# A hybrid DeltaNet and gMLP step: where the scan scales its operands, how its triangular inverse is joined, and how the modulation sums are laid on the array

## The chip, the cores and the metric

The kernel runs on one core of one Trainium2 chip. The metric is the device time of one execution in microseconds (us); less is better. The engines are named as the profile names them: PE (matrix engine; PEld its weight loads), DVE (vector), ACT (scalar), POOL (GpSimd), SP (the queue that issues DMAs). PSUM tiles are banks of 128 partitions x 512 f32.

## What is computed

One layer of a transformer-like step over 2176 tokens: 128 context tokens and 2048 latent tokens, d_model 1024. Half of the mixer is a gated DeltaNet of 4 heads x 128, run once forward and once backward, in f32:

```python
def step(S, xs):                      # one chunk
    qd, kd, u_c, w_c, qk_c, gl = xs
    v_new = u_c - einsum('ck,kv->cv', w_c, S)
    o = einsum('ck,kv->cv', qd, S) + einsum('cs,sv->cv', qk_c, v_new)
    S = S * exp(gl) + einsum('ck,cv->kv', kd, v_new)
    return S, o
```

Here `qd = q * exp(g)` and `kd = k * exp(g_last - g)` with g the running sum of the log decay within the chunk, a number per token and head. `u` and `w` come from a triangular solve with (I + A), A strictly lower, made of `k_beta k^T` times the decay. The outputs of both directions are added. Around it stand the other half of the mixer (a chunked gMLP), the shared input and output projections, adaLN modulation (six rows of 1024 for each of two conditions, `silu(cond) @ w_mod + b_mod`) and a squared-ReLU MLP of width 4096.

## The kernel before

The program is written for one core and recorded by a tile framework, whose scheduler then sets the order of the instructions on every engine from its own estimates; buffers of a pool are waited for where the next use begins. It has three stages, all bounded by matrix work: the input projection, convolution and q, k, v of all tokens (0 to 460 us of the profile), the scan with gMLP and output projection as filling work (460 to 1245 us), and the MLP.

**The scan.** It works on tiles of 128 tokens, 17 tiles forward and 17 backward, 34 units (`unit`, L985). Each unit has a list of preparation steps and a list of scan steps. A table of numbers, WINDOWS (L59), says at what time, counted in units, each step is recorded (L1386 to L1396); the filling work is spread over the same axis, so that PE always has independent products between the steps of the chain. A unit takes some 22 us.

Loads: `prep_loads` (L997) brings a row of g, broadcast to all partitions (`gb`, by `load_rows`, L973), and the products K K^T and Q K^T, which the first stage has written. `scan_loads` (L1004) brings k by token (`kt`), k and q by feature (`kT`, `qT`), v (`vt`) and a second broadcast row, `eg`, the exponential of g. Both kinds of row share a pool tag of three buffers. The rows are made in the first stage by `decay_steps` (step f4, L700), which transposes g and stores it to `g_d`, and its exponential to `eg_d`. The tables `eglg` = exp(g_last - g), `neg2` = -2 exp(g), `egl` = exp(g_last) hold a column for each tile, direction and head.

Preparation inverts I + A in f16 by doubling: blocks of 2, 4, 8, 16, 32 (`level`, L1050), each with one set of four products on the whole array (L1065), a masked eviction on DVE (L1069), then two sets of four (L1077, L1079) and two evictions on ACT (L1080, L1081). The last join, from blocks of 64 to 128 (L1091 to L1107), addresses quarters of the array: operands and results are slices of 64 partitions (`ra`, `rb`), L1095 is 64x64, and so are L1103 and L1105, which have different output halves. Then come a residual correction (L1113, L1114) and the inverse T (L1122 to L1125).

The scan steps of a unit (L1127 to L1174) are:

1. ACT scales `kt` by `eglg` (four heads, L1130). PE multiplies kT by the state S, DVE turns that into the right-hand side in `vt` (L1135).
2. PE multiplies T by `vt`; ACT copies the result to `vn` (L1143).
3. PE multiplies `kt` by `vn`; DVE adds it to the decayed state (L1155). DVE multiplies `qT` by `eg` (L1157).
4. PE accumulates, head by head, qT times S (L1166) and QK times `vn` (L1167) in one bank. Forward, ACT copies it to `o` (L1170) and it is stored; backward, DVE adds the forward output to it (L1173) and the output projection's steps take it.

**The modulation sums.** Seven column blocks of the modulation (jc 5 to 11) are made on DVE: each of two accumulators `acc` holds, for one condition, 128 partial sums by 512 columns, one per partition. `total` (L262) adds the partitions up by two f32 products with a stationary operand of two columns (`pick`, L265), adds the bias on DVE (L268) and stores the row. Five calls lie in the first stage, two in the MLP.

Of the kernel before, what the change touches and what calls it, by code (L numbers as in the profile page):

```python
# [23 lines left out]
H = 4  # L24
# [39 lines left out]
def hybrid_step(  # L64
# [37 lines left out]
    eg_d = dp.tile([NT * 8, P], F32, name="eg_d")  # L102
# [133 lines left out]
    def mod_steps(jc, pool, stage=None, psum=None, pair=None):  # L236
# [25 lines left out]
        def total():  # L262
            ps = (psum or pm1)()
            for c, acc in enumerate(u["acc"]):
                T.matmul(ps[0:2, :], pick[:, c, :], acc, start=c == 0, stop=c == 1)  # L265
            row = pair()[0][0:2, :] if pair else pool.tile([2, 512], F32, tag="mrow", name="mrow", bufs=1)
            load(out=row, in_=b_mod[0:1, jc * 512 : (jc + 1) * 512].to_broadcast([2, 512]))
            V.tensor_tensor(out=row, in0=ps[0:2, :], in1=row, op=ALU.add)  # L268
            store(out=mod_d[:, jc * 512 : (jc + 1) * 512], in_=row)
# [7 lines left out]
    with ExitStack() as ph:  # L277
# [365 lines left out]
        def decay_steps():  # L643
# [56 lines left out]
            def f4():  # L700
# [7 lines left out]
                erow = c["x"][1][:, 512:768]  # L708
                A.activation(erow[:, 0:P], pr[:, 0:P], AF.Exp)
                A.activation(erow[0:8, P:], pr[0:8, P : 2 * P], AF.Exp)  # L710
                for dst, src in ((g_d, grow), (eg_d, erow)):
                    store(out=dst[0:P, :], in_=src[:, 0:P])
                    store(out=dst[P:136, :], in_=src[0:8, P:])
# [232 lines left out]
    with ExitStack() as ph:  # L946
# [26 lines left out]
        def load_rows(src, t, d):  # L973
            gb = q32("gb", 3)
# [6 lines left out]
        pms = {s: f16(f"P{s}") for s in (2, 4, 8, 16, 32)}  # L981
# [3 lines left out]
        def unit(t, d):  # L985
# [18 lines left out]
            def scan_loads():  # L1004
# [6 lines left out]
                u["eg"] = load_rows(eg_d, t, d)  # L1011
# [79 lines left out]
            @prep.append  # L1091
            def _():
                p = pd()
                for h in range(H):
                    T.matmul(p[ra, h, 0:64], u["AH"][rb, h, ra], u["Y"][rb, h, rb], start=True, stop=True)  # L1095
                u["P"] = f16("Pm", 1)
                A.activation(u["P"][ra, :, 0:64], p[ra, :, 0:64], AF.Copy, scale=-1.0)

            @prep.append
            def _():  # L1100
                py, px = pd(), pd()
                for h in range(H):
                    T.matmul(py[ra, h, 0:64], u["X"][ra, h, ra], u["P"][ra, h, 0:64], start=True, stop=True)  # L1103
                for h in range(H):
                    T.matmul(px[rb, h, 0:64], u["P"][ra, h, 0:64], u["X"][ra, h, ra], start=True, stop=True)  # L1105
                V.tensor_copy(u["Y"][ra, :, rb], py[ra, :, 0:64])
                A.copy(u["X"][rb, :, ra], px[rb, :, 0:64])  # L1107
# [18 lines left out]

            @scan.append  # L1127
            def _():
                for h in range(H):
                    A.activation(u["kt"][:, h, :], u["kt"][:, h, :], AF.Copy, scale=col(eglg, h))  # L1130
                if u["s"] is not None:
                    p = pd()
                    quad(p, u["kT"], u["s"])
                    for h in range(H):
                        V.scalar_tensor_tensor(out=u["vt"][:, h, :], in0=p[:, h, :], scalar=col(neg2, h),  # L1135
                                               in1=u["vt"][:, h, :], op0=ALU.mult, op1=ALU.add)

            @scan.append
# [7 lines left out]
            def _():  # L1146
                s = u["s"]
                p = pd()
                quad(p, u["kt"], u["vn"])
# [3 lines left out]
                else:  # L1153
# [3 lines left out]
                    V.tensor_tensor(out=u["qT"], in0=u["qT"], in1=u["eg"], op=ALU.mult)  # L1157
# [3 lines left out]
            def _():  # L1161
                s = u["s"]
                p = pd()
                for h in range(H):
                    if s is not None:
                        T.matmul(p[:, h, :], u["qT"][:, h, :], s[:, h, :], start=True, stop=False)  # L1166
                    T.matmul(p[:, h, :], u["QK"][:, h, :], u["vn"][:, h, :], start=s is None, stop=True)  # L1167
                o = q32("o", 2)
                if d == 0:
                    A.copy(o, p)  # L1170
                    store(out=of_d[t * P : (t + 1) * P, :].rearrange("p (h d) -> p h d", h=H), in_=o)
                else:
                    V.tensor_tensor(out=o, in0=p, in1=u["of"].rearrange("p (h d) -> p h d", h=H), op=ALU.add)  # L1173
                    u["o"] = o  # L1174
# [775 lines left out]
```

## Time and profile before

| | |
|---|---|
| runs | 2615.22, 2618.3, 2622.74 us; median 2618.3 |
| profiled execution | 2614.33 us; its span, first to last instruction, 2612.6 us |
| PE busy | 2572.1 us, 98%, 15424 matmul records |
| DVE busy | 1778.0 us, 68% |
| ACT busy | 1237.3 us, 47% |
| POOL busy | 229.9 us, 9% |
| DMA | 580.86 MB, mean 222 GB/s |
| granted TensorE clock, mean | 0.995 |

The profile is one execution, and its times are its own. A row of instructions names the line, the engine, the operation, out<-in, the partitions and elements of both, the count, then the busy time in total, the mean ns of one, and the idle time of the engine just before them with what ended it. Matmul records overlap: a product's own duration includes its way through the array, so what it costs in a row of products is read from one start to the next. An f32 product shows as two records of the same line, an f32r or f16 product as one. "Granted clock" is 1.00 when PE ran at its full clock.

### The profile page before, as it was taken

What the parts mean: (1) busy time and instruction counts of PE and PEld (TensorE: products, weight loads), DVE (VectorE), ACT (ScalarE), POOL (GpSimd) and SP (SyncE); (2) the same over time, 40 slices, a digit from 0 to 9 for tenths busy, and PEclk for the clock granted to TensorE, in tenths of its full rate; (3) what the DMA queues carried; (4) which work ended last, traced back from release to release, by engine and by line L of the source; (5) the groups of instructions that cost most, each with busy time, mean ns of one, the idle gap of its engine ahead of it and who ended that gap; (6) DMA issues with size and microseconds to landing.
All of it is one profiled execution on the core that took longest, in us unless ns stands there. A gap on an engine that the chain in (4) does not pass through costs nothing.

```text
span 2612.6 us, 44469 instructions
## 1 busy us (share of the span) xinstructions
PE 2572.1 (98%) x15424; PEld 2157.7 (83%) x15424; DVE 1778.0 (68%) x3677; ACT 1237.3 (47%) x3074; POOL 229.9 (9%) x448
## 2 busy tenths in 40 slices
PE   9999999899999999999999999999999999999998
PEld 5999999688888777778888888888888887888887
DVE  5867746766666878885678876666675557775874
ACT  4755555655555757763355543333342432233451
POOL 3112112211111111110000000000000000000000
PEclk9999999899999999999999999999999999999999
DMA  8967637645445657784868789444479979786782
GB/s 282 313 204 221 193 114 243 233 143 174 160 160 170 219 180 265 266 303 155 289 208 260 235 270 313 115 117 121 125 232 376 321 271 318 264 253 214 239 263 89
DMA packets 499751, 580.86 MB, mean 222 GB/s; under 512 B 35692, under 2 KB 298268, under 8 KB 495942
## 3 DMA queue, kind: packets, MB, share of 16 engines
q1 hardware_dynamic: 499526, 578.03, 68.1%
q8 instruction: 121, 1.98, 0.3%
q14 instruction: 104, 0.85, 0.1%
HBM read 398.14 MB, written 179.74 MB: 221 GB/s over the span
## 4 chain that ended last, share of the span: by engine, by line
PE 86%; DMA 6%; DVE 4%; ACT 1%; issue 1%; POOL 0%; SPq 0%; DVEq 0%; POOLq 0%; ACTq 0%
PE f L227 16%; PE f L229 16%; PE f L228 16%; PE pj L227 6%; PE pj L229 6%; PE pj L228 6%; PE pd L995 3%; PE f L1590 2%; PE pm L227 2%; PE pm L229 1%; PE pm L228 1%; DMA raw<-in_w_mod_dram 1%; PE pt L607 1%; PE pd L1166 1%; PE pd L1167 1%
## 5 line engine op out<-in xcount | busy, mean ns | idle before, releaser
L227 PE MATMUL f<-hop,zH 128*128 128x512 f32 x960 | 373.4, 389 | 1.2 <-ACT zH L1476 1.2
L229 PE MATMUL f<-hop,zL 128*128 128x512 f32 x960 | 373.4, 389 | 0.0
L228 PE MATMUL f<-hop,zH 128*128 128x512 f32 x960 | 373.3, 389 | 0.0
L227 PE MATMUL f<-hop,wH 128*128 128x512 f32 x896 | 355.3, 397 | 0.2 <-issue 0.2
L228 PE MATMUL f<-hop,wH 128*128 128x512 f32 x896 | 349.1, 390 | 0.0
L229 PE MATMUL f<-hop,wL 128*128 128x512 f32 x896 | 347.9, 390 | 0.0
L1476 ACT CAST zH<-zraw 128x512 fp32r<-128x512 f32 x240 | 147.1, 620 | 288.1 <-DMA zraw<-s_d 94.4
L227 PEld LDWEIGHTS f<-hop,zH 128*128 128x128 f32 x960 | 180.2, 188 | 39.8 <-ACT zH L1476 1.6
L229 PEld LDWEIGHTS f<-hop,zL 128*128 128x128 f32 x960 | 180.2, 188 | 38.4 <-issue 0.9
L228 PEld LDWEIGHTS f<-hop,zH 128*128 128x128 f32 x960 | 180.2, 188 | 38.3 <-issue 0.9
L1470 DVE TENSOR_TENSOR zL<-zraw,zH 128x512 fp32r<-128x512 f32 x240 | 163.2, 688 | 68.4 <-ACT zH L1476 54.6
L229 PEld LDWEIGHTS f<-hop,wL 128*128 128x128 f32 x896 | 168.2, 188 | 35.2
L227 PEld LDWEIGHTS f<-hop,wH 128*128 128x128 f32 x896 | 168.5, 188 | 33.1 <-issue 0.9
L228 PEld LDWEIGHTS f<-hop,wH 128*128 128x128 f32 x896 | 168.5, 188 | 32.4
L227 PE MATMUL pj<-kH,wH 128*128 128x386 f32 (+2 forms) x568 | 190.4, 338 | 1.7 <-ACT junk L583 1.1
L229 PE MATMUL pj<-kH,wL 128*128 128x386 f32 (+2 forms) x568 | 189.7, 334 | 0.0
L228 PE MATMUL pj<-kL,wH 128*128 128x386 f32 (+2 forms) x568 | 189.0, 334 | 0.0
L184 POOL TENSOR_TENSOR r<-rsq,nhalf 128x1 f32<-128x1 f32 (+1 forms) x38 | 24.2, 637 | 1422.6 <-DVE rsq L183 1422.6
L553 DVE SCALAR_TENSOR_TENSOR cv<-pj,vec,cv 128x384 f32<-128x384 f32 (+2 forms) x164 | 87.1, 539 | 53.3 <-ACT cv L550 51.9
L227 PEld LDWEIGHTS pj<-kH,wH 128*128 128x128 f32 x568 | 107.0, 189 | 7.3 <-issue 4.7
L1476 ACT CAST wH<-s 128x512 fp32r<-128x512 f32 x96 | 59.4, 621 | 105.5 <-DVE s L1470 105.0
L228 PEld LDWEIGHTS pj<-kL,wH 128*128 128x128 f32 x568 | 107.4, 189 | 0.5
(396 smaller groups left out, 5748.0 us busy)
## 6 DMA issues: line engine op xcount, KB each, us to landing
zraw<-z_d SPq DMA_DIRECT2D x212, 256.0 KB
raw<-in_w_ff_dram SPq DMA_DIRECT2D x128, 256.0 KB
hop<-hop_d SPq DMA_DIRECT2D x28, 1024.0 KB
z_d<-c SPq DMA_DIRECT2D x96, 256.0 KB
zraw<-s_d SPq DMA_DIRECT2D x96, 256.0 KB
raw<-in_w_mod_dram SPq DMA_DIRECT2D x80, 256.0 KB
r<-in_w_ff_dram SPq DMA_DIRECT2D x80, 256.0 KB
s_d<-s SPq DMA_DIRECT2D x64, 256.0 KB
```

The costliest lines, as they stand in the source:

```text
L184: G.tensor_tensor(out=out, in0=t[:np_, :n], in1=nhalf[:np_, :n], op=ALU.pow)
L227: T.matmul(ps, lh, rh, start=first and i == 0, stop=False, skip_group_check=more)
L228: T.matmul(ps, lh, rl, start=False, stop=False, skip_group_check=more)
L229: T.matmul(ps, ll, rh, start=False, stop=last and i == n - 1, skip_group_check=more)
L553: V.scalar_tensor_tensor(out=cv[:, o : o + m], in0=ps[:, s + sh : s + sh + m], scalar=convw[:, w, j : j + 1], in1=cv[:, o : o + m], op0=AL ...
L607: T.matmul(ps[:, i * P : (i + 1) * P], kTt[:, i * P : (i + 1) * P], rhs[:, i * P : (i + 1) * P], start=True, stop=True)
L995: T.matmul(p[:, h, :], lhs[:, h, :], rhs[:, h, :], start=True, stop=True)
L1166: T.matmul(p[:, h, :], u["qT"][:, h, :], s[:, h, :], start=True, stop=False)
L1167: T.matmul(p[:, h, :], u["QK"][:, h, :], u["vn"][:, h, :], start=s is None, stop=True)
L1470: V.tensor_tensor(out=out, in0=a, in1=b, op=op)
L1476: A.copy(h, src)
L1590: T.matmul(ps[:, c : c + P], self.raw[m, kh][:, kp, :], x0[kh][:, kp, :], start=first and kp == 0, stop=last and kp == 3)
```

## The change

Four edits.

1. **Scan.** `kt` and `qT` stay as loaded. Step 1 multiplies S from both kT and qT; ACT scales the second result by `neg2` into `o` (`scaled`, four heads). Step 2 makes two tiles from T times `vt`: `vs`, scaled by `eglg` on DVE, and `vn`, copied by ACT. Step 3 multiplies `kt` by `vs`. Step 4 multiplies QK by `vn` alone, and DVE adds -0.5 times `o`: forward in one pass, backward in two (with the forward output, then with the bank).
2. **Decay rows.** `eg_d`, its two exponentials and two stores, and its load in each unit are gone; the row tag has two buffers.
3. **Join.** The last join uses the whole array like the levels below it: P has a 128x128 tile of its own (`pms[64]`, zeroed once), and all partitions take part; the zero blocks add nothing. The two results share one bank.
4. **Sums.** Each 512-column product becomes four of 128 columns, whose outputs lie at partitions 0, 32, 64 and 96; DVE adds the bias in four pieces.

```diff
@@ total
-                T.matmul(ps[0:2, :], pick[:, c, :], acc, start=c == 0, stop=c == 1)
+                for g in range(4):
+                    T.matmul(ps[32 * g : 32 * g + 2, 0:P], pick[:, c, :], acc[:, g * P : (g + 1) * P], start=c == 0,
+                             stop=c == 1)
...
-            V.tensor_tensor(out=row, in0=ps[0:2, :], in1=row, op=ALU.add)
+            for g in range(4):
+                sl = slice(g * P, (g + 1) * P)
+                V.tensor_tensor(out=row[:, sl], in0=ps[32 * g : 32 * g + 2, 0:P], in1=row[:, sl], op=ALU.add)
@@ f4
-                erow = c["x"][1][:, 512:768]
-                A.activation(erow[:, 0:P], pr[:, 0:P], AF.Exp)
-                A.activation(erow[0:8, P:], pr[0:8, P : 2 * P], AF.Exp)
-                for dst, src in ((g_d, grow), (eg_d, erow)):
-                    store(out=dst[0:P, :], in_=src[:, 0:P])
-                    store(out=dst[P:136, :], in_=src[0:8, P:])
+                store(out=g_d[0:P, :], in_=grow[:, 0:P])
+                store(out=g_d[P:136, :], in_=grow[0:8, P:])
@@ load_rows and the scan's tiles
-            gb = q32("gb", 3)
+            gb = q32("gb", 2)
...
-        pms = {s: f16(f"P{s}") for s in (2, 4, 8, 16, 32)}
+        pms = {s: f16(f"P{s}") for s in (2, 4, 8, 16, 32, 64)}
+        V.memset(pms[64], 0.0)
@@ scan_loads
-                u["eg"] = load_rows(eg_d, t, d)
@@ the join
-                    T.matmul(p[ra, h, 0:64], u["AH"][rb, h, ra], u["Y"][rb, h, rb], start=True, stop=True)
-                u["P"] = f16("Pm", 1)
-                A.activation(u["P"][ra, :, 0:64], p[ra, :, 0:64], AF.Copy, scale=-1.0)
+                    T.matmul(p[:, h, 0:64], u["AH"][:, h, :], u["Y"][:, h, rb], start=True, stop=True)
+                A.activation(pms[64][ra, :, rb], p[ra, :, 0:64], AF.Copy, scale=-1.0)
...
-                    T.matmul(py[ra, h, 0:64], u["X"][ra, h, ra], u["P"][ra, h, 0:64], start=True, stop=True)
+                    T.matmul(p[:, h, 0:64], u["X"][:, h, :], pms[64][:, h, rb], start=True, stop=True)
                 for h in range(H):
-                    T.matmul(px[rb, h, 0:64], u["P"][ra, h, 0:64], u["X"][ra, h, ra], start=True, stop=True)
-                V.tensor_copy(u["Y"][ra, :, rb], py[ra, :, 0:64])
-                A.copy(u["X"][rb, :, ra], px[rb, :, 0:64])
+                    T.matmul(p[:, h, 64:P], pms[64][:, h, :], u["X"][:, h, ra], start=True, stop=True)
+                V.tensor_copy(u["Y"][ra, :, rb], p[ra, :, 0:64])
+                A.copy(u["X"][rb, :, ra], p[rb, :, 64:P])
@@ scan steps
+            def scaled(out, p, table):
+                for h in range(H):
+                    A.activation(out[:, h, :], p[:, h, :], AF.Copy, scale=col(table, h))
...
-                for h in range(H):
-                    A.activation(u["kt"][:, h, :], u["kt"][:, h, :], AF.Copy, scale=col(eglg, h))
...
+                    p = pd()
+                    quad(p, u["qT"], u["s"])
+                    u["o"] = q32("o", 2)
+                    scaled(u["o"], p, neg2)
...
+                u["vs"] = q32("vs", 1)
+                cols = eglg[:, t, d * 4 : d * 4 + 4].unsqueeze(2).to_broadcast([P, 4, P])
+                V.tensor_tensor(out=u["vs"], in0=p, in1=cols, op=ALU.mult)
...
-                quad(p, u["kt"], u["vn"])
+                quad(p, u["kt"], u["vs"])
...
-                    V.tensor_tensor(out=u["qT"], in0=u["qT"], in1=u["eg"], op=ALU.mult)
...
-                for h in range(H):
-                    if s is not None:
-                        T.matmul(p[:, h, :], u["qT"][:, h, :], s[:, h, :], start=True, stop=False)
-                    T.matmul(p[:, h, :], u["QK"][:, h, :], u["vn"][:, h, :], start=s is None, stop=True)
+                quad(p, u["QK"], u["vn"])
...
+                    o = u["o"]
+                    V.scalar_tensor_tensor(out=o, in0=o, scalar=-0.5, in1=of if d else p, op0=ALU.mult, op1=ALU.add)
+                    if d:
+                        V.tensor_tensor(out=o, in0=o, in1=p, op=ALU.add)
```

What the scheduler makes of it is seen in the order of the instructions. First PE at the second join step of one forward unit, before (the last quarter products of each kind; X, Pm and pd are the tiles of the code):

```order
L1065 MATMUL pd<-Y,AH 128x64
L1103 LDWEIGHTS X
L1103 MATMUL pd<-Pm,X 64x64
...
L1105 LDWEIGHTS Pm
L1105 MATMUL pd<-X,Pm 64x64
L227 MATMUL pm<-wH,hH 128x512
L228 MATMUL pm<-wL,hH 128x512
```

and the same place after (P_5795 is `pms[64]`):

```order
L1064 MATMUL pd<-Y,AH 128x64
L1101 LDWEIGHTS X
L1101 MATMUL pd<-P_5795,X 128x64
...
L1103 LDWEIGHTS P_5795
L1103 MATMUL pd<-X,P_5795 128x64
L226 MATMUL pm<-wH,hH 128x512
L227 MATMUL pm<-wL,hH 128x512
```

The place among the neighbours is the same, and the number of products too; only their form differs. Next PE at the first modulation sum, before:

```order
L596 MATMUL pt<-ident,kn 128x128 x3
L229 MATMUL pj<-kH,wL 128x386
L265 MATMUL pm<-acc,pick 2x512 x2
L227 MATMUL pj<-kH,wH 128x386
L228 MATMUL pj<-kL,wH 128x386
```

and after:

```order
L599 MATMUL pt<-ident,kn 128x128 x3
L228 MATMUL pj<-kH,wL 128x386
L265 MATMUL pm<-acc,pick 2x128 x8
L226 MATMUL pj<-kH,wH 128x386
L227 MATMUL pj<-kL,wH 128x386
```

The eight short products stand together where the two long ones stood. Last, the query product on PE, before, in step 4 of one unit:

```order
L227 MATMUL pj<-wH,hH 128x512
L228 MATMUL pj<-wL,hH 128x512
L229 MATMUL pj<-wH,hL 128x512
L1166 MATMUL pd<-S,qT 128x128
L1167 MATMUL pd<-vn,QK 128x128
L1166 MATMUL pd<-S,qT 128x128
L1167 MATMUL pd<-vn,QK 128x128
```

and after, in step 1, behind the key product:

```order
L1259 MATMUL pm<-vg,wsT 128x128 x2
L995 MATMUL pd<-S,kT 128x128 x2
L995 MATMUL pd<-S,qT 128x128 x4
L1076 LDWEIGHTS X
L1076 MATMUL pd<-P_5792,X 128x64
```

It has moved ahead by three scan steps and is no longer interleaved with the product over `vn`, which stands alone as `L995 MATMUL pd<-vn,QK 128x128 x4`. DVE in the backward half works between the preparation's masks (L1069 before, L1068 after) and the output projection's pieces (`opL`, `tmp`, `x`). Before, in one unit:

```order
L1173 TENSOR_TENSOR o<-pd,of 128x512
L1048 TENSOR_TENSOR AL<-KK,AH 128x512
L890 TENSOR_TENSOR opL<-y,opH 128x512
...
L1039 TENSOR_TENSOR X<-AH,bd_182 128x512
L1157 TENSOR_TENSOR qT<-qT,gb 128x512
L1306 TENSOR_TENSOR r_14814<-r_14814,oss 128x4
L895 TENSOR_TENSOR ev<-ev,y 128x512
```

and in one unit after:

```order
L1179 SCALAR_TENSOR_TENSOR o<-o,of 128x512
L182 TENSOR_SCALAR rsq<-r_14807 128x4
L1032 SCALAR_TENSOR_TENSOR KK<-KK,beta,Es 128x128
L889 TENSOR_TENSOR opL<-y,opH 128x512
L1032 SCALAR_TENSOR_TENSOR KK<-KK,beta,Es 128x128 x3
...
L1314 TENSOR_TENSOR r_16295<-rq 128x4
L1148 TENSOR_TENSOR vs<-pd,eglg 128x512
L889 TENSOR_TENSOR opL<-y,opH 128x512
```

The scaling of qT is gone from that queue; `o<-o,of` has come ahead of the addition of the bank, and `vs` stands among the work of other units.

More of the change, by code (lines that the diff above doesn't have):

```diff
@@ L101, in hybrid_step @@
     g_d = dp.tile([NT * 8, P], F32, name="g_d")
-    eg_d = dp.tile([NT * 8, P], F32, name="eg_d")
     of_d = dp.tile([NTOK, 512], F32, name="of_d")
@@ L1136, in _ @@
                                                in1=u["vt"][:, h, :], op0=ALU.mult, op1=ALU.add)
+                    p = pd()
+                    quad(p, u["qT"], u["s"])
+                    u["o"] = q32("o", 2)
+                    scaled(u["o"], p, neg2)
             @scan.append
```

15 lines of the change are left out of this document (8 added, 7 removed).

## The prediction

> **What bounds the kernel now.** I read the page first (span, engines, the chain that ended last), then the busy time of the engines by stage, then the waits inside the scan, then single stretches of the timeline. From the page:
>
> ```profile
> span 2612.6 us, 44469 instructions
> PE 2572.1 (98%) x15424; PEld 2157.7 (83%) x15424; DVE 1778.0 (68%) x3677; ACT 1237.3 (47%) x3074; POOL 229.9 (9%) x448
> ...
> PE 86%; DMA 6%; DVE 4%; ACT 1%; issue 1%; POOL 0%; SPq 0%; DVEq 0%; POOLq 0%; ACTq 0%
> ```
>
> The matrix engine is busy for 98% of the span and holds 86% of the last chain, so what shortens its own work shortens the kernel, and what the others do counts only where it makes PE wait. The windows by stage (PE busy, then weight loads, DVE, ACT, POOL, granted clock, DMA share, GB/s) are the projection, the scan's start, its forward and its backward half, and the MLP:
>
> ```profile
> 0.00:460.00 460.00, 453.11 (x2689) 406.80 (x2689) 298.34 (x680) 250.97 (x742) 98.25 (x282) 1.00 0.73 226
> 460.00:500.00 40.00, 33.47 (x231) 24.21 (x228) 29.92 (x73) 25.48 (x67) 10.07 (x12) 0.79 0.75 262
> 500.00:880.00 380.00, 375.61 (x3207) 310.29 (x3206) 251.08 (x719) 209.69 (x558) 48.43 (x64) 1.00 0.52 166
> 880.00:1245.00 365.00, 352.57 (x3038) 287.71 (x3037) 278.36 (x711) 238.24 (x729) 54.58 (x65) 1.00 0.70 235
> 1300.00:2612.00 1312.00, 1302.50 (x6023) 1083.72 (x6021) 885.37 (x1439) 497.06 (x949) 17.57 (x26) 1.00 0.71 230
> ```
>
> PE is idle for 6.5 us at the scan's start, 4.4 us in the forward half and 12.4 us in the backward half. DVE is busy for 66% of the forward half (251.08 of 380) and 76% of the backward half (278.36 of 365). Cover is thinnest in the backward half, but there is some everywhere.
>
> **The join (34 units, two steps each).** Timeline of PE around the two join steps of one unit (start, duration, instruction):
>
> ```profile
> 711.04 0.28 PE L1077 MATMUL pd<-P,X 128*128 128x64 f16 x4
> 711.16 0.28 PE L1079 MATMUL pd<-X,P 128*128 128x64 f16 x4
> 711.38 0.31 PE L1095 MATMUL pd<-Y,AH 64*64 64x64 f16 x4
> 711.61 1.16 PE L995 MATMUL pd<-vn,kt 128*128 128x128 f32 x8
> ...
> 714.68 0.29 PE L1065 MATMUL pd<-Y,AH 128*128 128x64 f16 x4
> 714.90 0.21 PE L1103 MATMUL pd<-Pm,X 64*64 64x64 f16 x1
> 714.92 0.21 PE L1105 MATMUL pd<-X,Pm 64*64 64x64 f16 x1
> ...
> 715.03 0.19 PE L1105 MATMUL pd<-X,Pm 64*64 64x64 f16 x1
> 715.16 0.50 PE L227 MATMUL pj<-wH,hH 128*128 128x512 f32 x1
> ```
>
> Read start to start. Four full-array products of 64 columns take 0.12 us when the next group is full-array too (711.04 to 711.16). The same four take 0.22 us when a 64*64 product follows (711.16 to 711.38, 714.68 to 714.90), and the four quarter-size products of L1095 take 0.23 us before PE goes on. So the array loses about 0.1 us each time it enters the 64*64 form and again when it leaves. First step now: 0.22 + 0.23 = 0.45 us, against 2 groups x 0.12 = 0.24 us afterwards: 0.21 saved. Second step: 0.22 + 0.26 = 0.48 us, against three full-array groups, 0.36 us: 0.12 to 0.13 saved, although the eight quarter products now overlap in pairs (0.02 us from L1103 to L1105). Together 0.34 us a unit, times 34 = **11.5 us off PE**. The evictions keep their count and size; two bank tiles become one.
>
> The Trainium skill, TensorEngine Tiling (Array Packing), sections Theoretical Speedup and When to Use Tiling, speaks against this edit: it says to cut the array into tiles when contraction and columns are 64 or fewer, for up to twice the speed. The same page, Key Properties, has the other side, that changing the tiling mode drains TensorE. The gaps above agree with the second, which outweighs the first here because every tiled run is only four or eight products long.
>
> **The sums (7 calls, five before 460 us, two near 2170 and 2208 us).** PE around one of them, and a run of ordinary f32 products:
>
> ```profile
> 2169.16 0.39 PE L229 MATMUL f<-hop,zL 128*128 128x512 f32 x1
> 2169.48 1.88 PE L265 MATMUL f<-macc,pick 128*2 128x512 f32 x4
> 2171.29 0.50 PE L227 MATMUL f<-hop,zH 128*128 128x512 f32 x1
> ...
> 710.16 1.05 PE L1250 MATMUL pm<-vg,wsT 128*128 128x128 f32 x8
> ```
>
> Two f32 products appear as four passes, 1.81 us from 2169.48 to 2171.29. A pass of 128 columns takes 0.11 us (710.16 to 711.04, eight passes). The change makes 16 passes of 128 columns, four column groups per accumulator. One after the other they cost 16 x 0.11 + 0.09 for leaving the narrow form = 1.85 us, no gain. All four groups at once would be 4 x 0.11 + 0.09 = 0.53 us, 1.28 us saved a call, 9.0 us in seven. The nearest row for overlap is the L1103/L1105 pair, quarter products with different outputs that start 0.02 us apart. But each f32 product's two passes use the same columns and stand behind each other, so only the second pass of a group can run beside the first of the next: 8 x (0.11 + 0.02) + 0.09 = 1.13 us, 0.68 us saved a call. I take that, **4.8 us**, between bounds of 0 and 9.0. The one DVE addition of 512 columns becomes four short ones that write a row for a later stage; no one waits for it.
>
> **The scan's vector work.** The rows that price it (busy total, mean ns, idle before it and the releaser):
>
> ```profile
> L1157 DVE TENSOR_TENSOR qT<-qT,gb 128x512 f32<-128x512 f32 x32 | 22.7, 710 | 25.0 <-DMA qT<-qT_d 24.8
> L1173 DVE TENSOR_TENSOR o<-pd,of 128x512 f32<-128x512 f32 x16 | 11.0, 688 | 4.8 <-PE pd L1167 4.8
> L1130 ACT ACTIVATE kt<-kt,eglg 128x128 f32<-128x128 f32 x136 | 43.7, 393 | 36.4 <-DMA kt<-kt_d 33.1 <-PE pd L1105 2.9
> L1125 ACT ACTIVATE T<-pd,hbeta 128x128 f32<-128x128 f32 x136 | 38.8, 372 | 4.9 <-PE pd L995 4.6
> L1170 ACT COPY o<-pd 128x512 f32<-128x512 f32 x17 | 9.8, 575 | 1.9 <-PE pd L1167 1.7
> ```
>
> and one of the DMA queue's waits (us in total, times, longest):
>
> ```profile
> SPq L976 <- DVE qT L1157: 26.7, 17, 5.4
> ```
>
> DVE, per unit: the qT scaling goes (-0.71), the scaling of new values comes (+0.69, as L1173, PSUM in), and one pass over the output comes (+0.69), in the forward half instead of an ACT copy, in the backward half on top of L1173. Net +0.67 us a unit, 11 us in each half: DVE goes to about 69% and 79%. ACT: four kt scalings (4 x 0.393) are replaced by four output scalings (4 x 0.372), and 17 copies of 0.58 us go. What ACT and DVE stood waiting for loads in those two rows (33.1 and 24.8 us) goes too, and with it the work queued behind: ACT's casts and DVE's masks of the preparation. On the DMA queue, 34 loads of decay rows and two stores go, with their waits for the qT scaling (26.7 us in total), so no load is issued later than now for this. PE has the same products as before: the query product stands behind the key product instead of beside L1167. Cover: PE's fill; without it the net DVE work would cost 11 us in the backward half. I take nothing; bounds are a gain of 5 us (waits for loads gone) and a loss of 11.
>
> The new wait is the state update's: its product now takes vs, made by DVE, where it took vn, copied by ACT. Behind it PE has all its fill. In the backward half:
>
> ```profile
> 1043.46 1.14 PE L995 MATMUL pd<-vt,T 128*128 128x128 f32 x8
> ...
> 1044.63 0.59 ACT L1143 COPY vn<-pd 128x512 f32<-128x512 f32 x1
> ...
> 1049.78 0.92 PE L995 MATMUL pd<-vn,kt 128*128 128x128 f32 x6
> ```
>
> vn is ready at 1045.22 and read at 1049.78, so DVE may come 4.5 us later at no cost. The added pass over the output waits for ACT's scaling and, in the backward half, for the load of the forward output; behind it DVE has the next units' masks, and PE waits for those. That is inside the 11 us bound. The query tile is read earlier in the unit, but it is also freed earlier for the load that follows two units later. The output tile lives from the first step on; two buffers carry two units.
>
> **The scan's start.** The first five-us windows, columns as above:
>
> ```profile
> 460.00:465.00 5.00, 3.15 (x10) 1.48 (x7) 4.87 (x10) 3.00 (x8) 3.93 (x3) 0.74 1.05 399
> 465.00:470.00 5.00, 1.49 (x14) 0.88 (x13) 3.25 (x7) 4.61 (x13) 0.36 (x1) 0.50 1.02 384
> 470.00:475.00 5.00, 3.94 (x22) 2.60 (x22) 4.30 (x14) 3.39 (x11) 1.90 (x3) 0.50 0.84 310
> ...
> 457.48 1.28 ACT L1020 ACTIVATE E<-gb,gcol 128x128 f32<-128x128 f32 x4 [7.22 <-DMA gb<-g_d]
> ```
>
> DMA is full here and ACT waits 7.22 us for decay rows. Two stores of 68 KB leave the queue ahead of them, and their issues alone held it from 440.39 to 441.12:
>
> ```profile
> 440.39 0.35 SPq L712 DMA_DIRECT2D eg_d<-scr  x1
> 440.83 0.29 SPq L713 DMA_DIRECT2D eg_d<-scr  x1
> ```
>
> The kt scalings also leave ACT there, and one DVE memset of about 0.35 us comes (half of L1173 for half the bytes, an estimate). I take **1 us** gained; bounds are a loss of 3 and a gain of 8, the clock's share (1 - 0.79 of 40 us = 8.4) if PE stayed awake.
>
> **Sum.** 11.5 + 4.8 + 1 = 17.3 us less. The profiled execution took 2614.3 us (span 2612.6 and 1.7 around it), which gives 2597.0. The median of the runs is 4.0 us above it, 2618.3, and so the forecast for the median is **2601.0 us**.
>
> **Rivals**, from the same median. A measurement of this kernel tells about 0.3% from no change, 7.9 us.
>
> *The sums don't overlap.* For: the f32 passes quoted start a whole pass apart, none beside another. Then 11.5 + 1 = 12.5 us: 2605.8.
>
> *More is gained.* The groups overlap fully (9.0) and the start stays short enough to keep the clock (8.4): 28.9 us, 2589.4. For: the 0.50 clock follows PE gaps at 465 that hang on loads and ACT. Against: the first AH, X, Y chain is unchanged. The Trainium skill, TensorE: Matmul & The Clock Gate, Part 1, puts the drop to half rate after an idle window of about 3.4 us; the 0.50 rows agree with half rate, and by that rule a slightly shorter gap could save the clock.
>
> *DVE becomes the bound of the backward half.* All of its 11 us comes out as PE waits: 17.3 - 11 = 6.3 us, 2612.0. For: 76% busy and PE's 12.4 us idle there. Against: DVE's own waits for qT go.
>
> *The full array costs what it computes.* If the 0.1 us gaps belonged to these products and not to the change of form, they would stay, and the second step would lose the overlap of its pairs, 0.1 us x 34 = 3.4 us more: 4.8 + 1 - 3.4 = 2.4 us gained, 2615.9. It is what the first rule of the page TensorEngine Tiling (the Trainium skill) would make of the edit. Against: the gap is seen on the full-array group ahead and on the narrow one alike.
>
> *Slower: the state update waits for DVE.* Its in-order queue would hold vs back by more than the 4.5 us of cover. Each us of PE wait costs 34; from 0.51 us a unit the gain is gone (17.3 / 34), from 0.74 us the kernel is measurably slower; at 1 us, 34 - 17.3 = 16.7 us lost, 2635.0. For: recurrence through DVE twice a unit. Against: 4.5 us of cover in the half where DVE is busiest.
>
> **How the numbers follow.** Chances: forecast 0.41, sums without overlap 0.20, more gained 0.12, DVE bound 0.14, full array costs 0.04, slower 0.09. Range 2588 to 2616: from the case with more gained to the two cases near no change; the slower case stays out, with part of the tails. Faster by over 0.3% (under 2610.4): 0.40 of the forecast, 0.18, 0.12 and 0.02 of the DVE case = 0.72. Slower (over 2626.2): 0.08. Within: 0.20.
>
> **What would show it.** Right: the products of the join have full-array rows and 0.12 us from group to group; the sum's row shows products that start 0.01 to 0.02 us apart and about 1.1 us for the call; PE's idle time in both halves stays within 5 us of 4.4 and 12.4; no wait of the product over kt for vs. Wrong: waits of PE for DVE's P or vs that grow by over 10 us in the backward half, or a call of the sums that still takes 1.8 us.

## The result, and the profile after

The changed kernel takes **2597.3 us** in the median of four runs (2593.7 to 2598.9), the kernel before 2620.1 us (2615.2 to 2622.7): a ratio of 0.9913, 95% interval 0.9901 to 0.9924, or 22.8 us less. The forecast was 2601.0, in a range of 2588 to 2616. The profiled execution of the changed kernel took 2598.9 us, its slowest; that of before was its fastest (2614.3). So two profiles laid side by side show 15.5 us, and the scan seems to have gained less than it did. A second profile of before (below) mends that.

The page of the changed kernel: span, engines, and the shares of the last chain.

```profile
span 2596.8 us, 44648 instructions
PE 2553.3 (98%) x15508; PEld 2156.5 (83%) x15508; DVE 1801.0 (69%) x3733; ACT 1220.9 (47%) x3048; POOL 228.8 (9%) x448
...
PE 87%; DVE 5%; DMA 4%; ACT 1%; issue 1%; POOL 0%; SPq 0%; DVEq 0%; POOLq 0%; ACTq 0%
```

PE's busy time fell by 18.8 us (2572.1 to 2553.3). PE still bounds the kernel. The windows by stage, columns as before: projection, the scan's start, its forward and its backward half, MLP.

```profile
0.00:454.50 454.50, 449.78 (x2746) 408.72 (x2747) 300.80 (x697) 253.03 (x742) 99.29 (x283) 1.00 0.74 229
454.50:500.00 45.50, 40.54 (x311) 30.63 (x311) 35.73 (x97) 26.43 (x67) 9.29 (x13) 0.89 0.64 211
500.00:870.00 370.00, 363.35 (x3143) 302.94 (x3142) 253.68 (x713) 194.67 (x533) 44.21 (x61) 1.00 0.51 158
870.00:1232.00 362.00, 345.24 (x3028) 285.88 (x3027) 289.73 (x724) 233.99 (x726) 58.41 (x65) 1.00 0.69 227
1286.00:2596.00 1310.00, 1300.72 (x6050) 1084.17 (x6048) 886.67 (x1446) 497.61 (x950) 16.60 (x26) 1.00 0.71 231
```

The scan runs from 454.5 to 1232.0, 777.5 us, and PE is idle in it for 5.0, 6.6 and 16.8 us. DVE is at 69% of the forward half (253.68 of 370) and 80% of the backward half (289.73 of 362), as forecast. The join in the timeline (start, duration, instruction), the first step and then the second:

```profile
704.22 0.28 PE L1078 MATMUL pd<-X,P 128*128 128x64 f16 x4
704.34 0.28 PE L1094 MATMUL pd<-Y,AH 128*128 128x64 f16 x4
704.46 0.47 PE L995 MATMUL pd<-vs,kt 128*128 128x128 f32 x2
...
707.51 0.29 PE L1064 MATMUL pd<-Y,AH 128*128 128x64 f16 x4
707.64 0.28 PE L1101 MATMUL pd<-P,X 128*128 128x64 f16 x4
707.76 0.28 PE L1103 MATMUL pd<-X,P 128*128 128x64 f16 x4
707.87 0.47 PE L226 MATMUL pj<-wH,hH 128*128 128x512 f32 x1
```

Every group follows the one ahead of it by 0.11 to 0.13 us, and no pause stands at either end. A sum in the MLP:

```profile
2155.91 0.39 PE L228 MATMUL f<-hop,zL 128*128 128x512 f32 x1
2156.23 0.62 PE L265 MATMUL f<-macc,pick 128*2 128x128 f32 x16
2156.78 0.50 PE L226 MATMUL f<-hop,zH 128*128 128x512 f32 x1
```

Sixteen passes take 0.55 us from 2156.23 to 2156.78, where four long ones took 1.81. That is the full overlap of four column groups, which I had as the bound: 1.26 us a call, 8.8 us if all seven calls stood whole. They don't: the scheduler puts other products into three of the five calls of the first stage, so that these take 0.85 to 0.96 us. All seven together take 4.9 us of PE, against 12.8 before (in each piece, from its first pass to the next product): 7.9 less. PE's longest waits in the scan (total us, times, longest), and what DVE and ACT now do there:

```profile
PE pd L1076 <- DVE P L1068: 11.1, 13, 1.6
PE pd L1064 <- ACT Y L1079: 8.1, 12, 1.5
```

```profile
L1148 DVE TENSOR_TENSOR vs<-pd,eglg 128x512 f32<-128x512 f32 x34 | 23.1, 679 | 5.5 <-PE pd L995 5.5
...
L1179 DVE SCALAR_TENSOR_TENSOR o<-o,of 128x512 f32<-128x512 f32 x16 | 11.8, 739 | 1.0 <-ACT o L1127 1.0
```

PE waits for the solve's P and Y, and never for vs. The same two rows of the kernel before, in its second profile (below):

```profile
PE pd L1077 <- DVE P L1069: 12.0, 18, 1.9
PE pd L1065 <- ACT Y L1080: 5.5, 8, 1.3
```

Together these two waits have not become shorter: 17.5 us before, 19.2 after.

### The profile page after: what moved, and what is told of

Same layout as the page of the kernel before. It is cut to its first block, busy times and chain, and to the rows that moved or that the text cites. A ratio compares the mean times of both kernels' runs of the same rounds, so it can differ in the third digit from the quotient of the medians.

```text
span 2596.8 us, 44648 instructions
## 1 busy us (share of the span) xinstructions
PE 2553.3 (98%) x15508; PEld 2156.5 (83%) x15508; DVE 1801.0 (69%) x3733; ACT 1220.9 (47%) x3048; POOL 228.8 (9%) x448
## 4 chain that ended last, share of the span: by engine, by line
PE 87%; DVE 5%; DMA 4%; ACT 1%; issue 1%; POOL 0%; SPq 0%; DVEq 0%; POOLq 0%; ACTq 0%
PE f L226 16%; PE f L228 16%; PE f L227 16%; PE pj L226 7%; PE pj L228 7%; PE pj L227 7%; PE pd L995 5%; PE f L1599 2%; PE pm L226 1%; PE pm L227 1%; PE pm L228 1%; PE pt L610 1%; PE pt L569 1%; DMA QK<-qk_d 1%; PE pd L1076 1%
```

## The experiments

All ratios are to the kernel before, run on the same chip; the intervals are 95%. Two ratios of different kernels are clearly apart (95%) only from a distance of some 0.0018 to 0.002, about 5 us, so I put the times beside PE's busy and idle time in the scan, read from windows that cover it whole.

**The kernel before once more.** No edit.

> The kernel before once more, for a second profile of it: the first was its fastest execution (2614.3 us against a median of 2621). If that one was an unusually good scan, PE's idle time in the scan is here about 30 us, as in the profiles with the join or the sums alone (31.6 and 31.5), not 23.3. If the edits themselves added idle time, it is about 23 again.

It took 2619.9 us. Its windows (start, forward, backward):

```profile
460.00:500.00 40.00, 33.11 (x227) 23.96 (x228) 29.54 (x71) 25.07 (x65) 9.44 (x11) 0.79 0.77 269
500.00:880.00 380.00, 374.74 (x3196) 309.44 (x3196) 250.79 (x722) 208.67 (x556) 49.19 (x65) 1.00 0.52 166
880.00:1251.40 371.40, 354.86 (x3056) 289.39 (x3054) 279.55 (x712) 240.31 (x733) 54.66 (x65) 1.00 0.70 231
```

The scan takes 791.4 us with 28.7 us of idle PE (6.9, 5.3 and 16.5), 5.4 us more than in the windows of the profile that the forecast was made from (6.5, 4.4 and 12.4). So the first profile had a lucky scan, and the idle time after (28.4 us) is no rise at all. It also means that a difference of some 5 us in idle time between two single profiles says little by itself. The comparisons below use this second profile.

**The join alone.** From the kernel before:

```diff
-T.matmul(p[ra, h, 0:64], u["AH"][rb, h, ra], u["Y"][rb, h, rb], start=True, stop=True)
+T.matmul(p[:, h, 0:64], u["AH"][:, h, :], u["Y"][:, h, rb], start=True, stop=True)
...
-T.matmul(py[ra, h, 0:64], u["X"][ra, h, ra], u["P"][ra, h, 0:64], start=True, stop=True)
+T.matmul(p[:, h, 0:64], u["X"][:, h, :], pms[64][:, h, rb], start=True, stop=True)
...
-T.matmul(px[rb, h, 0:64], u["P"][ra, h, 0:64], u["X"][ra, h, ra], start=True, stop=True)
+T.matmul(p[:, h, 64:P], pms[64][:, h, :], u["X"][:, h, ra], start=True, stop=True)
```

> The kernel before with the join edit alone (34 units). Theory: the time is lost where the array changes between its full form and the 64*64 form, about 0.1 us each time, so full-array products save 0.34 us a unit, 11.5 us: a ratio of 0.9956, near 2608 us from a median of 2620. Rival (the gap belongs to these products whatever their form, and the pairs lose their overlap): 3.4 us slower, 1.0013. In the trace the narrow rows go, and PE passes from the first join step to the next group in 0.12 us.

Measured: 0.9972 (0.9960 to 0.9983), 7.3 us faster. Its scan in three windows:

```profile
460.00:500.00 40.00, 31.83 (x224) 23.07 (x225) 29.29 (x69) 25.98 (x68) 9.38 (x10) 0.79 0.81 282
500.00:880.00 380.00, 374.18 (x3247) 311.73 (x3245) 254.03 (x730) 213.58 (x568) 49.32 (x65) 1.00 0.52 167
880.00:1245.30 365.30, 346.01 (x3011) 284.96 (x3009) 276.64 (x706) 235.90 (x722) 55.26 (x65) 0.99 0.69 234
```

PE's busy time in the scan fell by 10.7 us (762.7 to 752.0), and its idle time rose by 4.6 (28.7 to 33.3). In the records of all 34 units, the time from the last product ahead of the join to the first behind it fell by 0.215 us in the first step and 0.113 in the second (medians): 0.328 a unit, 11.2 us, nearly my 11.5. So PE saved what was forecast. Part of it may have come back as waiting, but a rise of 4.6 us is within what two profiles of one kernel differ by, and the next experiment shows none.

**A join of half the width.** The changed kernel, with all 128 rows contracted but only 64 columns of the array used:

```diff
-T.matmul(p[:, h, 0:64], u["AH"][:, h, :], u["Y"][:, h, rb], start=True, stop=True)
+T.matmul(p[ra, h, 0:64], u["AH"][:, h, ra], u["Y"][:, h, rb], start=True, stop=True)
...
-T.matmul(p[:, h, 0:64], u["X"][:, h, :], pms[64][:, h, rb], start=True, stop=True)
+T.matmul(p[ra, h, 0:64], u["X"][:, h, ra], pms[64][:, h, rb], start=True, stop=True)
...
-T.matmul(p[:, h, 64:P], pms[64][:, h, :], u["X"][:, h, ra], start=True, stop=True)
+T.matmul(p[rb, h, 64:P], pms[64][:, h, rb], u["X"][:, h, ra], start=True, stop=True)
```

> The changed kernel, with the join's products contracting over all 128 rows but making only 64 output columns of the array (128*64 form). If any change of form costs about 0.1 us on the way in and out, whichever of the two sides is cut, the join's two steps lose 0.2 to 0.4 us a unit again: 7 to 13 us slower than the changed kernel, about 0.994 to 0.996 of before. If only the cut of the contraction (or the 64*64 pairing) costs, it is the same as the changed kernel, 0.991, and the gaps in the trace stay at 0.12 us a group.

Measured: 0.9955 (0.9940 to 0.9969), 2607.9 us, which is 0.0042 or 11.0 us above the changed kernel, with an error of about 5. PE's busy time in the scan is 12.4 us above the changed kernel's (761.6 against 749.1), and its idle time about the same (27.7 against 28.4): here all that PE lost came out as time. Both steps of one unit in the timeline:

```profile
708.24 0.28 PE L1078 MATMUL pd<-X,P 128*128 128x64 f16 x4
708.45 0.31 PE L1094 MATMUL pd<-Y,AH 128*64 128x64 f16 x4
708.69 0.94 PE L995 MATMUL pd<-vs,kt 128*128 128x128 f32 x6
...
711.76 0.29 PE L1064 MATMUL pd<-Y,AH 128*128 128x64 f16 x4
711.98 0.22 PE L1101 MATMUL pd<-P,X 128*64 128x64 f16 x1
711.99 0.22 PE L1103 MATMUL pd<-X,P 128*64 128x64 f16 x1
...
712.11 0.20 PE L1103 MATMUL pd<-X,P 128*64 128x64 f16 x1
712.24 0.50 PE L226 MATMUL pj<-wH,hH 128*128 128x512 f32 x1
```

The gaps are back: 0.21 and 0.24 us around the first step, 0.22 us ahead of the second, although nothing is cut but the columns, and although the second step's pairs run beside each other again. In the records of all 34 units the two steps take 0.30 us longer than in the changed kernel (medians), 10.3 us. The pause belongs to the change of form, not to the 64*64 products. The Trainium skill, TensorEngine Tiling (Array Packing), section Key Properties, says that changing the tiling mode drains TensorE; the runs agree with a pause at each change, of about 0.1 us each way here.

**The sums alone.** From the kernel before, for each accumulator:

```diff
-T.matmul(ps[0:2, :], pick[:, c, :], acc, start=c == 0, stop=c == 1)
+for g in range(4):
+    T.matmul(ps[32 * g : 32 * g + 2, 0:P], pick[:, c, :], acc[:, g * P : (g + 1) * P], start=c == 0,
+             stop=c == 1)
```

> The kernel before with the column-group sums alone (7 calls). Theory, from the trace of after: the four groups run fully beside each other, a call falls from 1.81 to about 0.55 us, 8.8 us in all: a ratio of 0.9966. As I forecast it (half overlapped): 4.8 us, 0.9982. No overlap: 1.000. Since five of the seven calls stand before the scan, about 6 us of the gain should be there by the scan's first product.

Measured: 0.9976 (0.9966 to 0.9986), 6.3 us faster, between the two expectations. In its trace the first product of the scan stands 4.9 us earlier than in the first profile of before.

**The sums in one column group.** The changed kernel:

```diff
-for c, acc in enumerate(u["acc"]):
-    for g in range(4):
-        T.matmul(ps[32 * g : 32 * g + 2, 0:P], pick[:, c, :], acc[:, g * P : (g + 1) * P], start=c == 0,
+for g in range(4):
+    for c, acc in enumerate(u["acc"]):
+        T.matmul(ps[0:2, g * P : (g + 1) * P], pick[:, c, :], acc[:, g * P : (g + 1) * P], start=c == 0,
                  stop=c == 1)
```

> The changed kernel, with the four parts of each sum in one and the same column group (partitions 0:2 of the output, four column ranges of the bank, one range after the other) instead of four column groups. The products have the same number and size. If the concurrency of the column groups is the whole gain of the sums, a call goes back to about 1.8 us and the kernel is 7 x 1.26 = 8.8 us slower than the changed one, about 0.9945 of before. If shorter passes alone were the gain, it stays at 0.991.

Measured: 0.9941 (0.9927 to 0.9955), 2604.6 us, 7.3 us above the changed kernel. One call:

```profile
2158.36 0.39 PE L228 MATMUL f<-hop,zL 128*128 128x512 f32 x1
2158.68 1.91 PE L265 MATMUL f<-macc,pick 128*2 128x128 f32 x16
2160.51 0.50 PE L226 MATMUL f<-hop,zH 128*128 128x512 f32 x1
```

The same sixteen products take 1.83 us one behind the other, against 0.55. So shorter passes alone gain nothing: the sums' gain is the concurrency of the column groups.

**Join and sums, without the scan edit.** The two edits above on the kernel before.

> The kernel before with join and sums, without the scan edit. If the two are additive, 11.5 + 8.8 = 20.3 us less than before, 0.9923. If the scan edit costs up to 6 us, this kernel is at or below the changed one (0.9913 of before in its own comparison) although it has less in it, about 0.989 to 0.991; if the scan edit gains 3 us or more, it lies 3 us or more above the changed one, 0.9925 or higher.

Measured: 0.9953 (0.9939 to 0.9966), 12.4 us faster, where the two terms had made 20.3 and the two edits alone 13.6. This is some 10 us above the changed kernel, so the theory that the scan edit costs something falls, and the rival holds. Its scan:

```profile
455.00:500.00 45.00, 36.51 (x284) 27.13 (x284) 36.70 (x96) 28.69 (x74) 13.27 (x14) 0.89 0.71 245
500.00:875.00 375.00, 367.83 (x3175) 305.94 (x3174) 244.09 (x698) 208.13 (x555) 45.62 (x61) 1.00 0.52 167
875.00:1243.10 368.10, 347.60 (x3018) 285.75 (x3018) 277.71 (x709) 237.52 (x725) 55.24 (x65) 0.99 0.69 232
```

PE is idle for 36.2 us here (8.5, 7.2 and 20.5), and for 28.4 in the changed kernel (5.0, 6.6 and 16.8): by one profile of each, 7.8 of the scan's 10.6 us (788.1 to 777.5) are waits of PE that the scan edit took away, nearly half of them in its first 45 us. In PE's lists of waits those for P and Y are no shorter (18.4 us here, 19.2 in the changed kernel). Smaller are those for the scan's output on its way into the output projection (o and its rounded copy oH, 5.1 and 1.2) and for the inverse's X and R (3.4 and 0.3).

**The scan edit alone.** From the kernel before, its core:

```diff
-u["eg"] = load_rows(eg_d, t, d)
...
-A.activation(u["kt"][:, h, :], u["kt"][:, h, :], AF.Copy, scale=col(eglg, h))
...
+quad(p, u["qT"], u["s"])
+scaled(u["o"], p, neg2)
...
+V.tensor_tensor(out=u["vs"], in0=p, in1=cols, op=ALU.mult)
...
-V.tensor_tensor(out=u["qT"], in0=u["qT"], in1=u["eg"], op=ALU.mult)
```

> The kernel before with the scan edit alone (unscaled queries and keys, scaled outputs and new values, no decay rows, gb in two buffers). Theory: no gain worth naming, or a loss of some us, because DVE does 0.67 us more a unit and PE's idle time in the scan grew by about 5.6 us from before to after: 0 to 6 us slower, 1.000 to 1.0023. Rival: the loads waited for are gone and the scan's start is shorter, 3 to 5 us faster, 0.998 to 0.999.

Measured: 0.9967 (0.9955 to 0.9978), 8.7 us faster, more than either side had expected. With 7.3 and 6.3 for the others the three edits make 22.3 us one by one, and 22.8 together: within their intervals, they add up. (Its profiled execution was its slowest, 2616.0 against a median of 2611.7, so its trace shows little of the gain.)

**The query half alone, on join and sums.** Against the changed kernel, the key half is taken back:

```diff
+for h in range(H):
+    A.activation(u["kt"][:, h, :], u["kt"][:, h, :], AF.Copy, scale=col(eglg, h))
...
-V.tensor_tensor(out=u["vs"], in0=p, in1=cols, op=ALU.mult)
...
-quad(p, u["kt"], u["vs"])
+quad(p, u["kt"], u["vn"])
```

> Join and sums, and of the scan edit the query half alone: queries unscaled, outputs scaled, decay rows gone; keys are still scaled on ACT and the state update takes vn from ACT. Compared with the kernel of join and sums and with the changed kernel it splits the scan edit. If the added DVE work on the output is what costs, this kernel already lies above join and sums by 2 to 5 us; if the move of the state update to DVE's vs costs, it lies below the changed kernel by 2 to 5 us; if neither, all three are within 2 us.

Measured: 0.9934 (0.9918 to 0.9950), 2602.1 us. It lies midway between join and sums (0.9953) and the changed kernel (0.9913), about 5 us from each. The step from join and sums is within what the intervals leave open, the step to the changed kernel at the edge of it. Both halves seem to gain, and neither is seen to cost. ACT still waits for kt here, 58.5 us in total.

**The decay rows again, unused.** The kernel just above, with the rows made, stored and loaded into a buffer of their own:

```diff
-gb = q32("gb", 2)
+gb = q32("gb", 2) if src is g_d else q32("eg")
...
+load_rows(eg_d, t, d)
```

> Join, sums and the query half of the scan edit (2602.1 us in its own comparison, 0.9934 of before), with the decay rows made, stored and loaded again as in the kernel before, but into a buffer of their own that no instruction reads, so that no load waits for DVE. If the rows' own transfers (two stores ahead of the scan, 34 loads) are what the scan edit saves, the kernel goes back towards that of join and sums, 0.9953: 3 to 5 us slower than without them, with PE idle for about 8 us again in the first 50 us of the scan (4.7 without, 8.5 in join and sums). If it is the loads' wait for DVE or the work moved off the engines, it stays within 2 us of 0.9934.

Measured: 1.0094 (1.0080 to 1.0108), 2643.4 us, 41 us slower than without the rows. No theory had that. The load queue's waits (total, times, longest):

```profile
SPq L980 <- DMA eg<-eg_d: 73.5, 29, 3.1
```

and PE in 120 us of the scan, in this kernel,

```profile
500.00:620.00 120.00, 87.63 (x690) 73.19 (x689) 52.04 (x151) 47.68 (x133) 8.76 (x12) 0.84 0.54 163
```

and without the rows:

```profile
500.00:620.00 120.00, 118.61 (x1046) 99.49 (x1045) 81.52 (x241) 70.11 (x198) 14.74 (x20) 1.00 0.52 163
```

Two things differ from the kernel before. Nothing uses these rows, so the scheduler issued all 34 loads between 451 and 591 us, where the kernel before spreads them from 456 to 1158. And the single buffer made each of them wait, at the head of the queue, until the one before it had landed, so that the loads behind came late. PE stood idle for 31 us more there, and lost clock with it (0.84); half of that is a single stop of 15.5 us, in which ACT waited 15.4 us for kt. So the run is confounded: it doesn't price the rows' traffic as the kernel before has it. DMA was no fuller in these 120 us (0.54 and 163 GB/s, against 0.52 and 163). What it does show is how dear waits at the head of the load queue can be in this scan: 73.5 us of them go with a loss of about 41 us.

**vs on ACT.** The changed kernel:

```diff
-V.tensor_tensor(out=u["vs"], in0=p, in1=cols, op=ALU.mult)
+scaled(u["vs"], p, eglg)
```

> The changed kernel, with vs written by ACT (four scalings a unit) and not by DVE (one multiply): 0.69 us a unit less on DVE, about 1.5 us more on ACT. If DVE's load is what makes PE wait in the backward half, PE's idle time there falls and the kernel gains 2 to 5 us on the changed one; if cover is enough, no difference; if the latency of the state update counts (vs after vn in ACT's queue), it is 2 to 10 us slower.

Measured: 0.9898 (0.9882 to 0.9914), 2593.8 us, the fastest median of all; the 0.0015 below the changed kernel are within what two intervals leave open. Its scan:

```profile
453.40:500.00 46.60, 42.00 (x308) 31.63 (x308) 35.88 (x96) 28.51 (x73) 9.99 (x14) 0.85 0.62 212
500.00:870.00 370.00, 366.29 (x3167) 305.15 (x3166) 247.54 (x702) 212.68 (x604) 44.25 (x61) 1.00 0.51 160
870.00:1227.10 357.10, 341.50 (x3002) 284.09 (x3002) 276.38 (x702) 247.64 (x787) 59.09 (x65) 1.00 0.69 229
```

PE's idle time is 23.9 us (4.6, 3.7 and 15.6), 4.5 less than in the changed kernel, for 19 us less on DVE (three windows together, 579.1 to 559.8).

**More work on DVE.** The changed kernel, with a pass that changes nothing:

```diff
+V.tensor_tensor(out=o, in0=o, in1=o, op=ALU.max)
```

> The changed kernel with one more DVE pass a unit that changes nothing (the maximum of the output tile with itself, about 0.7 us, 34 times, 24 us of DVE work). The mirror of writing vs on ACT, which took 23.5 us off DVE and gave 3.5 us. If DVE's load sets PE's waits in the backward half at that rate, 3 to 5 us slower than the changed kernel (0.9925 to 0.993 of before); if DVE is at its bound there, up to 12 us in the backward half alone (0.996); if its cover is whole, no difference (0.991).

Measured: 0.9924 (0.9910 to 0.9937), 2599.5 us, 2.9 us above the changed kernel by the ratios, within what they leave open. The pass in the trace:

```profile
L1182 DVE TENSOR_TENSOR o<-o 128x512 f32<-128x512 f32 x33 | 22.7, 687 | 0.5
```

It adds 0.687 us a unit, 23 us, about as much as the whole scan edit adds in the two halves together, and the 11 us that it puts into the backward half do not come out as time: PE's idle time in the scan is 27.0 us, against 28.4. DVE has cover there. By this run and the one with vs on ACT, some 20 us of DVE work are worth 3 to 4 us either way, which is less than either can tell from nothing. But these two kernels lie 0.0026 or 6.8 us apart, with an error of 5.5, for 37 us of DVE work in the scan (559.8 and 596.4), so the cover is perhaps not whole; they differ in the engine that makes vs as well.

**The forward output added on GpSimd.** vs on ACT, and in the backward half:

```diff
-V.scalar_tensor_tensor(out=o, in0=o, scalar=-0.5, in1=of if d else p, op0=ALU.mult, op1=ALU.add)
 if d:
-    V.tensor_tensor(out=o, in0=o, in1=p, op=ALU.add)
+    G.tensor_tensor(out=o, in0=o, in1=of, op=ALU.add)
+V.tensor_tensor(out=o, in0=o, in1=p, op=ALU.add)
```

> The changed kernel with vs on ACT, and in the backward half the addition of the forward output on GpSimd, which is idle there, so that DVE has one pass over the output in both halves (the output's factor is taken without the -2). 0.69 us a unit less on DVE than with vs on ACT alone, in the backward half. If DVE's load still makes PE wait there, 1 to 4 us faster than vs on ACT alone (0.9898): 0.988 to 0.9895; if not, the same; if GpSimd's slower addition holds the output's tile or the store up, slower.

Measured: 0.9971 (0.9962 to 0.9981), 2611.7 us, 19 us slower than vs on ACT alone by the ratios. GpSimd's addition takes twice DVE's time:

```profile
L1180 POOL TENSOR_TENSOR o<-o,of 128x512 f32<-128x512 f32 x16 | 23.2, 1453 | 70.6 <-ACT o L1128 70.6
```

But the scan lost little: 775.9 us between its first and last product, against 773.7. About 14 us of the loss lie in the MLP, where the edit changes no instruction. A group of its products here,

```profile
L227 PE MATMUL f<-hop,zH 128*128 128x512 f32 x960 | 376.6, 393 | 1.2 <-ACT zH L1485 1.2
```

and with vs on ACT alone:

```profile
L226 PE MATMUL f<-hop,zH 128*128 128x512 f32 x960 | 373.4, 389 | 1.2 <-ACT zH L1484 1.2
```

Passes that read 512 columns in one piece start every 230.0 ns (mean over 2871), against 226.7 there, at the same granted clock of 1.00. It isn't the chip: the kernel with the extra DVE pass ran on the same one, also at 226.7. The edit's only reach into that stage is a table of 136 values (544 bytes) in each partition that it keeps for the output's factor, which shifts the tiles behind it. That an address matters here is a guess; it wasn't tried.

## Why the prediction was right, and where its sum was off

The time, the sign and the range held: 2597.3 against 2601.0. The closeness is in part luck. The gain was 22.8 us, where the sum had 17.3; the time came within 3.7 because the median of before was 1.8 us higher in the runs that the result is compared with. Of the three terms, the join was right, and the sums and the scan were too small.

- **What bounds the kernel.** Right. PE is at 98% before and after, and the chain's share of it went from 86 to 87%. The profile came from the shortest execution; by starting from the distance to the median, the forecast kept that out of its sum, but not out of its reading of idle time: 23.3 us in the scan's windows were 28.7 in the second profile.
- **The join: 11.5 us.** The mechanism is shown (a join of half the width loses 11.0 us again, with the same gaps), and PE's work shrank by 11.2. On the clock it was worth 7.3 us alone (4.5 to 10.5), and 11.0 with an error of about 5 when it was taken out of the changed kernel. The sum counted every microsecond off PE as time. With the scan edit in place the runs agree with that; whether part of it comes back as waiting without the scan edit, as the lower figure and the 4.6 us of idle time suggest, isn't shown.
- **The sums: 4.8 us, bounds 0 and 9.0.** Too low. The step that failed is "each f32 product's two passes use the same columns and stand behind each other, so only the second pass of a group can run beside the first of the next". In the program's order the four groups' passes overlap fully: 0.55 us a call that stands whole instead of 1.13, 7.9 us on PE with the split ones, 6.3 (3.7 to 8.9) and 7.3 on the clock by the two experiments.
- **The scan's vector work: 0, bounds a gain of 5 and a loss of 11; its start: 1, bounds -3 and +8.** The step that failed is "I take nothing", for the loads' waits. DVE went to 69% and 80% as forecast, and 23 us more on it cost 2.9 us with an error of about 5, so most of the loss at least was covered. But the gain was real: 8.7 us alone (5.8 to 11.8), some 10 on top of the others, inside the two bounds' sum of 13. By one profile of each, PE's idle time at the start fell by 3.5 us and in the backward half by 3.7 against join and sums.
- **The rivals.** Sums without overlap, DVE as the bound of the backward half, and a state update that waits for DVE are refuted by the call of 0.55 us, by the extra DVE pass, and by the waits of PE, which show no row for vs. The full array that costs what it computes, 2615.9, is refuted by the join of half the width: the narrower form was the dearer one. The rule of the Trainium skill, TensorEngine Tiling (Array Packing), section When to Use Tiling, did not pay here for runs of four products one behind the other and of eight in pairs. "More is gained" was right on the sums and half right on the clock: what it lost in the start fell from 8.4 us (0.21 of 40) to 5.0 (0.11 of 45.5), and was 5.0 in join and sums too, so that the scan edit need not have had a part in it. Each figure is one execution, and the start's clock is 0.84 to 0.85 in others (the scan edit alone, the query half, vs on ACT).

What stays open is which part of the scan edit frees PE. In the kernel before, ACT stood waiting for kt 33.1 us in total, DVE for qT 24.8, and the load queue for the qT scaling 26.7; all three rows are gone after. But others have come. ACT then waits 40.3 us for vs ahead of vn and 49.1 for the join's Y ahead of X (24.0 before, for the product), and the load queue waits 55.1 us for KK, where it waited 40.7 (second profile). So the rows that went don't explain the gain by themselves. The run with the query half alone puts about half of the gain on either side, within its error, and the run with the unused rows shows that a wait at the queue's head can be this dear, but not that this one was.

## What to carry to other kernels

Before you cut a small product to fit the array, look at what stands beside it: a run of four or eight products in a narrower form paid about 0.1 us on the way in and again on the way out, more than the narrow form saved, while four column groups kept busy side by side made one sum three times shorter. A scaling that sits between a load and its product ties an engine, a buffer and the load queue to that load; moved to the product's output it gained here even though it added work, and which of the three ties cost the time is open. And take a second profile before you read a few microseconds of idle time: here two executions of one kernel differed by 5 us in the scan alone.

## What the runs showed of the hardware

- With four f32 products of 128 columns on four column groups, four passes started 6 to 7 ns apart and the next four 88 to 90 ns behind, two such sets for each accumulator: both passes of an f32 product ran beside the other groups' passes. Sixteen passes took 0.55 us, on one group 1.83.
- A form of 128 rows by 64 columns pays the same pause as one of 64*64: 0.21 to 0.24 us where full-array groups follow each other in 0.12.
- The same 512-column f32 products ran 1.5% slower (230.0 against 226.7 ns from start to start) in a kernel whose only difference in that stage was 544 bytes more in each partition. It cost about 14 us and is not explained.
- GpSimd took 1.45 us for a 128x512 f32 addition that took DVE 0.69.
